# Layer-norm closings by full-array products at hand-set places, and 512-column products in the last feed-forward

## The chip, the cores and the metric

The kernel runs on one core of one Trainium2 chip. The metric is the device time of one execution in microseconds (us); less is better. A core has five engines with a queue of instructions each: TensorE (PE, matrix products), VectorE (DVE), ScalarE (ACT), GpSimd (POOL) and SyncE (SP, which here issues the DMA transfers). An engine works through its own queue in order, and waits at an instruction whose inputs, or whose buffers, aren't ready.

## The reference

Two layers of a transformer-like trunk over 256 context tokens and 256 latent tokens of width 1024. A layer is a SwiGLU feed-forward, a block of four token mixers in parallel, and a second feed-forward. Every one of these sub-layers is modulated and closed by a residual and a layer norm:

```
def modulate(h, mods, s):
    return h * (1 + mods[..., s, 1, :]) + mods[..., s, 0, :]
def residual(h, y, mods, s, g, b, r):
    return layer_norm(ALPHA * h + r * mods[..., s, 2, :] * y, g, b)
def swiglu_ffn(h, w_in, w_out):
    a = h @ w_in
    return (jax.nn.silu(a[..., :D_FF]) * a[..., D_FF:]) @ w_out
```

D_FF is 2816. All inputs are fp32, and only the latent tokens are returned, so the last sub-layers need the latent tokens alone.

## The kernel before

Channels lie on the 128 partitions and tokens along the free axis: eight tiles `ah[k]` of 128 channels by 512 columns hold the stream, columns 0 to 255 the context tokens (set 0), columns 256 to 511 the latent tokens (set 1). In the code `order` is (1, 0): the latent set comes first.

An fp32 product is made as three products in a faster format (fp32r). `split` turns a value into a rounded part and the rest: ScalarE writes `hi`, VectorE `lo`. A weight tile thus becomes `hi` and `lo`, an input tile `xh` and `xl` (in front of the first product of a sub-layer) or `gh` and its rest (in front of the second). `mm3` multiplies hi·hi, hi·lo and lo·hi into one PSUM tile; three such products are called a triple here. With both sets a triple has 512 columns, with one set 256. Split weights live in pools of six buffers (`hi`, `lo`), raw weights in four.

A feed-forward runs in three parts over 22 blocks of 128 hidden channels (`PARTS`). Per block it makes two product tiles of eight triples each (gate and up), then Silu on ScalarE, a product on VectorE and the split into `gh`. At the end of a part `out_tiles` multiplies the part's `gh` with the output weights into eight tiles, and `evac` adds each, times a gate, onto `ah[m]` (one `scalar_tensor_tensor`, `stt`, per set).

The layer norm is prepared while these last tiles arrive: `Norm.arrive` adds up the squares (`sq`) and the values (`lns`) of the eight tiles. `Norm.finish` closes it: products with a matrix of ones give the mean and the mean square of each token as rows (`st`, 32 equal rows per 128 tokens), ScalarE and VectorE work on a tile of 64 by 128 (`lnm`, `lnv`: copy, square, subtract, square root, reciprocal), and products with one column of the identity matrix, repeated, spread both rows over all 128 partitions (`bcm`, the mean, and `bcr`, the reciprocal deviation). Then `center` and `scale` on VectorE make the normalized tiles, ScalarE makes `xf` (the modulated tile), and the split gives `xh` and `xl`. `carry` multiplies `ah` for the next residual (the `ah<-ah,alg` instructions).

Between two sub-layers with both sets (four places: first feed-forward to mixers, mixers to second feed-forward, that to the next layer's first, and that to the second mixers) the last four output tiles are delayed (`LAG`): they are made for the latent set first, then for the context set (the late tiles), so that the latent closing lies beside the late tiles and the context closing beside the first products of the next sub-layer (the head). Behind the second mixers and behind the last feed-forward only the latent set is left, and the closing has no such company.

The order of instructions on each engine is set by the framework's scheduler, from the order in the code and its own costs.

Of the kernel before, what the change touches and what calls it, by code (L numbers as in the profile page):

```python
# [17 lines left out]
T = 256  # L18
# [16 lines left out]
HEAD = 3  # L35
PUMPS = ((3, 3), (3, 0), (3, 1))
# [24 lines left out]
def trunk_kernel(ctx: ExitStack, tc: tile.TileContext, I: dict, out: bass.AP):  # L61
# [81 lines left out]
    def mm3(ps, wh, wl, xh, xl, start, stop):  # L143
        mm(ps, wh, xh, start=start, stop=False)
        mm(ps, wh, xl, start=False, stop=False)
        mm(ps, wl, xh, start=False, stop=stop)
# [112 lines left out]
    class Norm:  # L259
# [3 lines left out]
        def __init__(self, n, tiles, pre=False):  # L263
            self.n, self.tiles, self.pre, self.bc = n, tiles, pre, {}

        def arrive(self, m, cs):
# [18 lines left out]
            if m == 0:  # L285
                self.q = sq
            else:
                if m == 1:
                    self.s = blk("lns")
                tt(out=self.q[:, cs], in0=self.q[:, cs], in1=sq[:, cs], op=ALU.add)  # L290
                tt(out=self.s[:, cs], in0=(self.tiles[0] if m == 1 else self.s)[:, cs], in1=d[:, cs], op=ALU.add)

        def finish(self, s):
# [3 lines left out]
            for i, x in enumerate((self.q, self.s)):  # L297
# [17 lines left out]

        def center(self, m, s, o):
# [7 lines left out]
    def xtiles():  # L324
        return ([xp.tile([128, 512], F32R, tag="xh", name=nm("xh")) for _ in range(8)],
                [xp.tile([128, 512], F32R, tag="xl", name=nm("xl")) for _ in range(8)])

    def start(mid):


        xh, xl = xtiles()
# [15 lines left out]
        for u in range(4):  # L347
# [15 lines left out]
            for k in (2 * u, 2 * u + 1):  # L363
# [15 lines left out]
                split(xh[k], xl[k], xf)  # L379
# [12 lines left out]
        return xh, xl, tiles  # L392
# [3 lines left out]
    class Boundary:  # L396
# [3 lines left out]
        def __init__(self, nrm, l, s, nl, ns_, keep, rest):  # L400
            self.nrm, self.ls, self.nx, self.keep, self.rest = nrm, (l, s), (nl, ns_), keep, rest
            self.xh, self.xl = xtiles()
            self.xf = {}

        def apply(self, v, ks):
            nrm = self.nrm
            c = vcols(v)
            for k in ks:
# [5 lines left out]
                split(self.xh[k][:, c], self.xl[k][:, c], xf[:, c])  # L414
# [16 lines left out]
        def prep(self, v):  # L431
            if v not in self.nrm.bc:
                self.nrm.finish(v)
                for k in range(HEAD):
                    self.nrm.center(k, v, ah[k])
                self.apply(v, range(HEAD))
                for k in range(HEAD, 8):
                    self.nrm.center(k, v, ah[k])
                for w, go in self.rest:
                    go()  # L440
                    self.nrm.finish(w)
                self.apply(v, range(HEAD, 8))
            else:
                for k in range(8):
                    self.nrm.center(k, v, ah[k])
                self.apply(v, range(8))

# [6 lines left out]
    def mmk(tiles, xh, xl, c):  # L454

        n = len(xh)
        for k in range(n):
            for p, wh, wl in tiles:
                mm3(p[:, c], ktile(wh, k), ktile(wl, k), xh[k][:, c], xl[k][:, c], k == 0, k == n - 1)

    def head_tiles(tiles, bd, order, cs):

        for v in order:
            if cs.start <= v * T:
                bd.prep(v)
                mmk(tiles, bd.xh, bd.xl, vcols(v))
        for v in order:
            if cs.start <= v * T:
                bd.carry(v)

    def out_tiles(load, gh, gl, cs, order, evac, lag):


        n = len(gh)
        for m in range(8 - lag):
            wh, wl = load(m)
            p = mmb()
            mmk([(p, wh, wl)], gh, gl, cs)
            evac(m, p, cs, order)
        late = []  # L480
# [3 lines left out]
        todo = []  # L484
        for i, v in enumerate(order if lag else ()):
            def go(v=v):
                for m, p, wh, wl in late:
                    mmk([(p, wh, wl)], gh, gl, vcols(v))
                    evac(m, p, vcols(v), (v,))

            if i:
                todo.append((v, go))
            else:
                go()
        return todo

    def resid(m, ps, l, s, sets):
# [26 lines left out]
    def ffn(l, w, bd, first, cs, order, np_, nm_=1):  # L524

        s = 2 * w
        nrm = Norm(1024, ah, True)
        xh, xl = first[:2] if bd is None else (bd.xh, bd.xl)
        rest = None
        for pi, (j0, j1) in enumerate(PARTS):  # L530
            gh, gl = [], []
            j = j0
            while j < j1:
                js = list(range(len(first[2]) // 2 if bd is None else 2)) if j == 0 else [j]
                tiles = first[2] if j == 0 and bd is None else ffn_tiles(l, w, js)
                if j == 0 and bd is not None:
                    head_tiles(tiles, bd, order, cs)
                elif j == 0:
                    mmk(tiles, xh, xl, cs)
                else:  # L540
                    for t in tiles:
                        mmk([t], xh, xl, cs)
                for i, jj in enumerate(js):
                    sg = blk("sg")
                    act(sg[:, cs], tiles[2 * i][0][:, cs], AF.Silu)
                    tt(out=sg[:, cs], in0=sg[:, cs], in1=tiles[2 * i + 1][0][:, cs], op=ALU.mult)
                    a, b = blk2("gh", cs, F32R)
                    split(a[:, cs], b[:, cs], sg[:, cs])
                    gh.append(a)
                    gl.append(b)  # L550
# [771 lines left out]
```

## Time and profile before

| what | value |
|---|---|
| median of 3 runs | 2264.93 us (2259.85 to 2268.72) |
| profiled execution | 2267.27 us, of which 2265.5 are the span of the trace |
| mean granted TensorE clock | 0.991 of full speed |
| VectorE busy | 1630.0 us, 72% of the span |
| ScalarE busy | 947.0 us, 42% |
| DMA | 323.23 MB, 143 GB/s on average |

The profile is of one execution. Busy time of an engine is the sum of its instructions; the span is from the first to the last instruction. Matmuls are pipelined: the duration of a row is longer than the distance to the next one, so the pace of products is read from their start times. A "granted clock" of 0.50 means that TensorE ran at 1.2 instead of 2.4 GHz in that stretch.

### The profile page before, as it was taken

How to read it: one execution, taken by the hardware profiler on the slowest of the kernel's cores; microseconds unless marked ns; L12 is line 12 of the kernel's file. 1: busy time of each engine (PE TensorE's matmuls, PEld its weight loads, DVE VectorE, ACT ScalarE, POOL GpSimd, SP SyncE). 2: the span in 40 equal slices, each digit the busy share in tenths (PEclk: the TensorE clock that was granted, in tenths of full speed). 3: DMA queues.
4: the chain of work that ended last, by engine and by line, in shares of the span. 5: the costliest groups of instructions: out<-in, count | busy, mean ns of one | idle time of the engine just before them, and what ended most of it. 6: DMA issues, size and time to landing. Idle time of an engine off the chain costs nothing.

```text
span 2265.5 us, 31565 instructions
## 1 busy us (share of the span) xinstructions
PE 2221.0 (98%) x12216; PEld 1908.4 (84%) x12216; DVE 1630.0 (72%) x2881; ACT 947.0 (42%) x1477; POOL 19.9 (1%) x82
## 2 busy tenths in 40 slices
PE   7999999999999999999999999999999999998997
PEld 4888788988888888898888888888889998998997
DVE  6998855768995754795746498766558988776656
ACT  5323123742345753362222254222226645755443
POOL 2000000000000000000000000000000000000000
PEclk9999999999999999999999999999999999999999
DMA  8676643223232132244545425554434543354652
GB/s 308 220 229 221 192 152 94 98 84 113 94 99 88 57 103 93 96 135 150 170 129 158 130 84 186 179 180 152 140 102 142 192 139 103 122 174 136 203 180 83
DMA packets 94454, 323.23 MB, mean 143 GB/s; under 512 B 10592, under 2 KB 12640, under 8 KB 94304
## 3 DMA queue, kind: packets, MB, share of 16 engines
q1 hardware_dynamic: 94304, 321.22, 43.9%
q8 instruction: 96, 1.57, 0.3%
q14 instruction: 54, 0.44, 0.1%
HBM read 320.12 MB, written 1.05 MB: 142 GB/s over the span
## 4 chain that ended last, share of the span: by engine, by line
PE 87%; DVE 7%; DMA 3%; issue 2%; ACT 2%; SPq 0%; DVEq 0%; ACTq 0%
PE mm L122 82%; DVE junk L216 2%; DMA ada<-in_wada 1%; DVE lo L113 1%; PE num L122 1%; DMA raw<-in_ffn_in 1%; DVE junk L366 1%; ACT hi L125 1%; DVE ah L113 0%; PE gt L122 0%; PE ax L122 0%; PE qk L122 0%; PE bcm L122 0%; PE bcr L122 0%; PE st L122 0%
## 5 line engine op out<-in xcount | busy, mean ns | idle before, releaser
L125 ACT ACTIVATE hi<-raw 128x1024 fp32r<-128x1024 f32 (+1 forms) x462 | 474.5, 1031 | 1040.0 <-PE mm L122 659.1
L122 PE MATMUL mm<-xh,hi 128*128 128x512 f32 (+1 forms) x2448 | 847.8, 349 | 5.0 <-ACT hi L125 3.0
L122 PE MATMUL mm<-xl,hi 128*128 128x512 f32 (+1 forms) x2448 | 850.0, 348 | 0.0
L122 PE MATMUL mm<-xh,lo 128*128 128x512 f32 (+1 forms) x2448 | 850.0, 348 | 0.0
L113 DVE TENSOR_TENSOR lo<-raw,hi 128x1024 fp32r<-128x1024 f32 (+1 forms) x462 | 546.2, 1185 | 264.6 <-ACT hi L125 262.4
L122 PEld LDWEIGHTS mm<-xh,hi 128*128 128x128 f32 x2448 | 462.4, 190 | 65.0 <-ACT hi L125 4.4
L122 PEld LDWEIGHTS mm<-xh,lo 128*128 128x128 f32 x2448 | 464.8, 190 | 58.8 <-DVE lo L113 0.4
L122 PEld LDWEIGHTS mm<-xl,hi 128*128 128x128 f32 x2448 | 465.2, 190 | 57.9 <-issue 0.7
L122 PE MATMUL mm<-gh,hi 128*128 128x512 f32 (+1 forms) x1600 | 405.8, 344 | 5.6 <-ACT gh L125 4.7
L216 DVE CUSTOM_DVE_ANT_0 junk<-ada,cbc 128x1024 bf16<-128x1024 f32 x256 | 312.9, 1222 | 107.1 <-DMA ada<-in_wada 104.0
L122 PEld LDWEIGHTS mm<-gh,hi 128*128 128x128 f32 x1600 | 276.6, 189 | 48.0 <-ACT gh L125 5.1
L122 PE MATMUL mm<-gh,lo 128*128 128x512 f32 (+1 forms) x800 | 275.5, 345 | 0.0
L122 PEld LDWEIGHTS mm<-gh,lo 128*128 128x128 f32 x800 | 150.8, 189 | 20.2 <-issue 0.7
L113 DVE SCALAR_TENSOR_TENSOR ah<-mm,gate,ah 128x256 f32<-128x256 f32 x192 | 86.4, 479 | 81.4 <-PE mm L122 81.2
L113 DVE SCALAR_TENSOR_TENSOR cacc<-pd,cw,cacc 128x512 f32<-128x512 f32 (+1 forms) x240 | 133.1, 613 | 0.2
L122 PE MATMUL mm<-yh,hi 128*128 128x512 f32 (+1 forms) x512 | 129.3, 339 | 0.1
L113 DVE TENSOR_TENSOR sg<-sg,mm 128x512 f32<-128x512 f32 (+1 forms) x87 | 53.7, 618 | 82.4 <-PE mm L122 81.7
L122 PEld LDWEIGHTS mm<-yh,hi 128*128 128x128 f32 x512 | 88.0, 189 | 11.6 <-ACT yh L125 0.3
L122 PE MATMUL mm<-yh,lo 128*128 128x512 f32 (+1 forms) x256 | 86.5, 338 | 0.0
L125 ACT ACTIVATE gh<-sg 128x512 fp32r<-128x512 f32 (+1 forms) x88 | 50.5, 574 | 76.0 <-DVE sg L113 75.5
L122 PE MATMUL mm<-mh,hi 128*128 128x256 f32 (+1 forms) x320 | 67.0, 306 | 0.5 <-ACT mh L125 0.3
L125 ACT ACTIVATE xf<-ah,bp,gp 128x256 f32<-128x256 f32 x88 | 48.8, 592 | 21.6 <-DVE ah L113 16.5
(241 smaller groups left out, 1759.6 us busy)
## 6 DMA issues: line engine op xcount, KB each, us to landing
raw<-in_ffn_in SPq DMA_DIRECT2D x176, 512.0 KB, 3.4
ada<-in_wada SPq DMA_DIRECT2D x136, 512.0 KB, 4.2
raw<-in_ffn_out SPq DMA_DIRECT2D x64, 512.0 KB, 3.7
raw<-in_w_G SPq DMA_DIRECT2D x64, 512.0 KB, 3.3
raw<-in_w_br SPq DMA_DIRECT2D x32, 512.0 KB, 3.3
raw<-in_ffn_out SPq DMA_DIRECT2D x32, 384.0 KB, 3.4
raw<-in_w_o SPq DMA_DIRECT2D x24, 512.0 KB, 3.4
shw<-in_wshift SPq DMA_DIRECT2D x16, 256.0 KB, 5.8
```

Of the source, the lines that this page charges most:

```text
L113: return f(*a, **k)
L122: nc.tensor.matmul(o, w, x, **kw)
L125: S.activation(o, i, f, **kw)
L216: V.tensor_tensor_reduce(out=cur["junk"], in0=w, in1=cur["c"][:, v], scale=1.0, scalar=0.0, op0=ALU.mult, op1=ALU.add, accum_out=m[:, v, t ...
L366: V.tensor_tensor_reduce(out=cur["junk"], in0=w, in1=cur["c"][:, v], scale=1.0, scalar=0.0, op0=ALU.mult, op1=ALU.add, accum_out=m[:, v, k ...
```

## The change

1. `finish` is replaced, between sub-layers and at the end, by `stats` and `spread` (the norm inside the mixers keeps `finish`). `stats` makes the mean by one product of the full ones matrix with `lns`, which leaves it on all partitions at once. The two sums per token are made with the tile as the weights and two columns of ones as the input, so that tokens lie on partitions; the square, the subtraction, the root and the reciprocal then work on a tile of 128 by 4 (`lnw`). Two `tensor_scalar` make a diagonal matrix of the result (`dg`), and `spread` multiplies it with the ones matrix.
2. Where only the latent set is left (`alone`), the last tile and its square are not added on VectorE but accumulated on TensorE as products of their own.
3. `head_tiles` writes the order of TensorE out by hand: after `GAP[0]` = 8 late triples `stats` of the latent set, 8 triples later `spread`, then the rest of the late triples; after 8 head triples `stats` of the context set, 8 later its `spread`.
4. In the last feed-forward the input tiles hold hi and lo side by side (`wide`), so hi·hi and hi·lo become one product of 512 columns; the two halves are added behind it, for gate and up by a copy on ScalarE and a sum on VectorE, for the output tiles by a second `stt`.

```
+        def stats(self, s):
+            n, cs = self.n, vcols(s)
+            b, c = aux("bcm"), aux("bcr")
+            for i, x in enumerate(self.s):
+                mm(b[:, 0:T], ones[n], x[:, cs], start=i == 0, stop=i == len(self.s) - 1)
+            ops = [(j, x, t) for i in range(len(self.q)) for j, x in ((0, self.q[i]), (1, self.s[i])) for t in range(2)]
+            for i, (j, x, t) in enumerate(ops):
+                o, k = T + 4 * j + 2 * t, s * T + t * 128
+                mm(c[:, o:o + 2], x[:, k:k + 128], ones[n][:, 0:2], start=i == 0, stop=i == len(ops) - 1)
+            e2, mu = c[:, T:T + 4], c[:, T + 4:T + 8]
...
+            act(v, mu, AF.Square)
+            tt(out=v, in0=e2, in1=v, op=ALU.subtract)
+            act(v, v, AF.Sqrt, bias=eps)
+            V.reciprocal(v, v)
+            dg = blk("dg")
+            for t in range(2):
+                ts(out=dg[:, t * 128:t * 128 + 128], in0=ident, scalar1=v[:, 2 * t:2 * t + 1], scalar2=float(n),
+                   op0=ALU.mult, op1=ALU.mult)
...
+        def spread(self, s):
+            mm(self.bc[s][1], ones[self.n], self.dg[:, 0:T], start=True, stop=True)
...
+        w, late = bd.rest
+        with tc.manual_schedule(engines={mybir.EngineType.PE}):
+            g = late()
+            some(g, GAP[0])
+            nrm.stats(v)
+            some(g, GAP[1])
+            nrm.spread(v)
...
+            for _ in g:
+                pass
+            bd.apply(v, range(HEAD, 8))
+            g = triples(tiles, xs, vcols(v))
+            some(g, GAP[0])
+            nrm.stats(w)
+            some(g, GAP[1])
+            nrm.spread(w)
...
+        if x.both is not None:
+            mm(ps, wh, x.both, start=start, stop=False)
+            mm(o, wl, hi, start=False, stop=stop)
...
+                    if wide:
+                        up = blk("up")
+                        for o, q in ((sg, 2 * i), (up, 2 * i + 1)):
+                            t = tiles[q][0]
+                            act(o[:, cs], t[:, 0:T], AF.Copy)
+                            tt(out=o[:, cs], in0=o[:, cs], in1=t[:, cs], op=ALU.add)
...
-            stt(out=ah[m][:, vcols(v)], in0=ps[:, vcols(v)], scalar=gate[l, s][:, v, m:m + 1],
-                in1=ah[m][:, vcols(v)], op0=ALU.mult, op1=ALU.add)
+            for c in ((vcols(0), vcols(v)) if wide else (vcols(v),)):
+                stt(out=ah[m][:, vcols(v)], in0=ps[:, c], scalar=gate[l, s][:, v, m:m + 1],
+                    in1=ah[m][:, vcols(v)], op0=ALU.mult, op1=ALU.add)
```

Three places show how the order moves. The first is the context closing between the first feed-forward and the mixers, on TensorE; `xh_2921` to `xh_2927` are input tiles of the latent set, `mm_` the head tiles (the change gives other numbers to the inputs: 2919, 2920, ... before, 2919, 2921, ... now). Before:

```order
L122 MATMUL mm_2972<-xl_2929,hi_2968 128x256
L122 MATMUL st_3132<-sq_2659,ones_81 32x128 x2
L122 MATMUL st_3132<-lns_2696,ones_81 32x128 x2
L122 MATMUL mm_2972<-xh_2921,lo_2969 128x256
...
L122 MATMUL mm_2958<-xl_2930,hi_2954 128x256
L122 MATMUL bcm_3139<-lnm_3137,ident 128x128 x2
...
L122 MATMUL mm_2972<-xh_2923,lo_2969 128x256
L122 MATMUL bcr_3140<-lnv_3138,ident 128x128 x2
L122 MATMUL mm_2951<-xh_2924,hi_2947 128x256
```

With the change:

```order
L123 MATMUL mm_2972<-xh_2921,lo_2969 128x256
L123 MATMUL bcm_3181<-lns_2696,ones_81 128x256
L123 MATMUL bcr_3182<-ones_81,sq_2659 128x2 x2
L123 MATMUL bcr_3182<-ones_81,lns_2696 128x2 x2
L123 MATMUL mm_2951<-xh_2923,hi_2947 128x256
...
L123 MATMUL mm_2972<-xh_2925,lo_2969 128x256
L123 MATMUL bcr_3182<-dg_3193,ones_81 128x256
L123 MATMUL mm_2951<-xh_2927,hi_2947 128x256
```

Three groups of products became two, with exactly eight triples between them; the second group stands ahead of the fifth input tile instead of behind the fifth.

The second place is ScalarE at the same boundary: `hi_` of a `raw_` is the split of a weight, `xf_` and `xh_` are the inputs of the latent set's head products, `lnm_3137`, `lnv_3138` and `lnw_3188` belong to the context closing. Before:

```order
L125 ACTIVATE xf_2994<-ah_102,bp_1294,gp_1293 128x256
L125 ACTIVATE hi_2968<-raw_2966 128x1024
L125 ACTIVATE xh_2919<-xf_2994 128x256
...
L125 ACTIVATE ah_104<-ah_104,alg_378 128x256
L125 ACTIVATE hi_3458<-raw_3456 128x1024
...
L125 ACTIVATE xf_3155<-ah_106,bp_1294,gp_1293 128x256
L125 ACTIVATE lnm_3137<-st_3132 64x128
L125 ACTIVATE xh_2923<-xf_3155 128x256
L125 ACTIVATE xf_3160<-ah_107,bp_1294,gp_1293 128x256
```

With the change:

```order
L126 ACTIVATE hi_2968<-raw_2966 128x1024
L126 ACTIVATE sq_3015<-ah_106 128x256
L126 ACTIVATE hi_3457<-raw_3455 128x1024
L126 ACTIVATE xf_3052<-ah_102,bp_1294,gp_1293 128x256
L126 ACTIVATE xf_3057<-ah_103,bp_1294,gp_1293 128x256
L126 ACTIVATE xh_2919<-xf_3052 128x256
...
L126 ACTIVATE xf_3152<-ah_109,bp_1294,gp_1293 128x256
L126 ACTIVATE lnw_3188<-bcr_3182 128x4
L126 ACTIVATE ah_105<-ah_105,alg_378 128x256
L126 ACTIVATE xh_2933<-xf_3152 128x256
L126 ACTIVATE lnw_3188<-lnw_3188,eps 128x4
```

The weight split of the next projection (`hi_3458`, now `hi_3457`) moved from behind the first three inputs to ahead of the first one, and the opening of the context closing from behind the fifth `xf` (`xf_3155`, of the tile `ah_106`) to behind the eighth.

The third place is ScalarE at the end of the first part of the last feed-forward, where the last block's gate (`sg`) and up values become `gh`; `mm_18027` and `mm_18034` are its two product tiles, `hi_` of 768 columns are splits of output weights. With the change:

```order
L126 ACTIVATE sg_18067<-mm_18027 128x256
L126 ACTIVATE hi_18164<-raw_18162 128x768
L126 ACTIVATE sg_18067<-sg_18067 128x256
L126 ACTIVATE hi_18185<-raw_18183 128x768
L126 ACTIVATE up_18068<-mm_18034 128x256
L126 ACTIVATE gh_18075<-sg_18067 128x256
```

Before, the same place read:

```order
L125 ACTIVATE hi_18261<-raw_18259 128x768
L125 ACTIVATE sg_18149<-mm_18093 128x256
L125 ACTIVATE hi_18287<-raw_18285 128x768
L125 ACTIVATE gh_18152<-sg_18149 128x256
L125 ACTIVATE hi_18313<-raw_18311 128x768
```

Two copies out of PSUM came in, and one more weight split now stands between the gate's copy and the last `gh`.

## Rows read from the trace of the kernel before

**Rows 1.** The page, first part: busy time, share of the span and instructions of each engine.
```profile
PE 2221.0 (98%) x12216; PEld 1908.4 (84%) x12216; DVE 1630.0 (72%) x2881; ACT 947.0 (42%) x1477; POOL 19.9 (1%) x82
```

**Rows 2.** Stretches: length; busy PE, PEld, DVE, ACT, POOL; granted clock; DMA share, GB/s.
```profile
22.20:25.80 3.60, 3.38 (x8) 2.46 (x9) 3.43 (x4) 2.41 (x5) 2.16 (x2) 0.53 1.04 386
398.00:426.00 28.00, 28.00 (x228) 26.28 (x227) 25.71 (x67) 21.52 (x47) 0.38 (x6) 1.00 0.12 39
2054.00:2062.00 8.00, 5.15 (x22) 4.86 (x23) 6.69 (x19) 5.38 (x13) 0.00 (x0) 0.50 0.13 51
```

**Rows 3.** Timeline of TensorE, last feed-forward: start, duration, engine, line, instruction, count.
```profile
2095.08 0.40 PE L122 MATMUL mm<-gh,hi 128*128 128x256 f32 x2
...
2096.86 0.96 PE L122 MATMUL mm<-gh,hi 128*128 128x256 f32 x4
2097.66 0.40 PE L122 MATMUL mm<-gh,lo 128*128 128x256 f32 x2
...
2149.90 0.28 PE L122 MATMUL mm<-xh,hi 128*128 128x256 f32 x1
...
2151.58 0.28 PE L122 MATMUL mm<-xh,lo 128*128 128x256 f32 x1
```

**Rows 4.** Timeline of TensorE, closings between first feed-forward and mixers.
```profile
401.72 0.71 PE L122 MATMUL bcr<-lnv,ident 64*128 64x128 f32 x4
402.36 0.38 PE L122 MATMUL mm<-gh,lo 128*128 128x256 f32 x1
...
414.28 0.41 PE L122 MATMUL st<-sq,ones 128*32 128x128 f32 x4
...
418.84 0.37 PE L122 MATMUL bcr<-lnv,ident 64*128 64x128 f32 x1
```

**Rows 5.** Timeline of ScalarE, same boundary.
```profile
404.42 1.06 ACT L125 ACTIVATE hi<-raw 128x1024 fp32r<-128x1024 f32 x1
405.39 0.40 ACT L125 ACTIVATE xh<-xf 128x256 fp32r<-128x256 f32 x1
405.70 1.08 ACT L125 ACTIVATE xf<-ah,bp,gp 128x256 f32<-128x256 f32 x2
406.68 0.71 ACT L125 ACTIVATE xh<-xf 128x256 fp32r<-128x256 f32 x2
407.30 1.57 ACT L125 ACTIVATE ah<-ah,alg 128x256 f32<-128x256 f32 x3
...
414.95 0.27 ACT L125 ACTIVATE lnm<-st 64x128 f32<-64x128 f32 x1
```

**Rows 6.** TensorE's waits, 18 to 26 us: who for what, total, times, longest.
```profile
PE mm L122 <- ACT hi L125: 2.5, 1, 2.5
```

**Rows 7.** Timeline of TensorE, 512-column products of the first feed-forward.
```profile
299.82 0.39 PE L122 MATMUL mm<-xh,hi 128*128 128x512 f32 x1
...
301.86 0.39 PE L122 MATMUL mm<-xh,hi 128*128 128x512 f32 x1
...
378.70 0.62 PE L122 MATMUL mm<-gh,hi 128*128 128x512 f32 x2
...
381.24 0.40 PE L122 MATMUL mm<-gh,lo 128*128 128x512 f32 x1
```

**Rows 8.** Timeline of all engines, the two one-set closings.
```profile
2049.43 0.28 PE L122 MATMUL mm<-mh,lo 128*128 128x256 f32 x1
...
2053.91 0.94 DVE L311 RECIPROCAL lnv<-lnv 64x128 f32<-64x128 f32 x1
...
2056.16 1.08 DVE L113 TENSOR_TENSOR ah<-ah,bcr 128x256 f32<-128x256 f32 x3 [0.71 <-PE bcr L122]
...
2058.07 1.22 PE L122 MATMUL mm<-xh,hi 128*128 128x256 f32 x4 [1.94 <-ACT xh L125]
...
2258.30 1.07 DVE L113 TENSOR_TENSOR ah<-ah,bcr 128x256 f32<-128x256 f32 x3
```

**Rows 9.** The products with `lf` in the mixers: what TensorE idled for, total, times.
```profile
  DVE lf L113: 4.2, 1
```

More of the change, by code (lines that the diff above doesn't have):

```diff
@@ L452, in ktile, with mmk, triples, some @@
         return w[:, k * 128:k * 128 + 128]
-    def mmk(tiles, xh, xl, c):
-        n = len(xh)
+    def mmk(tiles, xs, c):
+        for _ in triples(tiles, xs, c):
+            pass
+    def triples(tiles, xs, c):
+        n = len(xs)
         for k in range(n):
             for p, wh, wl in tiles:
-                mm3(p[:, c], ktile(wh, k), ktile(wl, k), xh[k][:, c], xl[k][:, c], k == 0, k == n - 1)
-    def head_tiles(tiles, bd, order, cs):
[L463 to L474, printed above, removed]
+                mm3(p, ktile(wh, k), ktile(wl, k), xs[k], c, k == 0, k == n - 1)
+                yield
+    def some(g, n):
+        for _ in range(n):
+            next(g, None)
+    def head_tiles(tiles, bd, order, cs):
+        nrm, xs = bd.nrm, bd.xs
+        v = order[0]
+        if not bd.rest:
+            nrm.stats(v)
+            nrm.spread(v)
+            for k in range(8):
+                nrm.center(k, v, ah[k])
+            bd.apply(v, range(8))
+            mmk(tiles, xs, vcols(v))
+            bd.carry(v)
+            return
+        w, late = bd.rest
+        with tc.manual_schedule(engines={mybir.EngineType.PE}):
+            g = late()
+            some(g, GAP[0])
+            nrm.stats(v)
+            some(g, GAP[1])
+            nrm.spread(v)
+            for k in range(8):
+                nrm.center(k, v, ah[k])
+            bd.apply(v, range(HEAD))
+            for _ in g:
+                pass
+            bd.apply(v, range(HEAD, 8))
[4 more added lines that the diff above has]
+            nrm.spread(w)
+            if cs.start <= w * T:
+                for k in range(8):
+                    nrm.center(k, w, ah[k])
+                bd.apply(w, range(8))
+            for _ in g:
+                pass
+            if cs.start <= w * T:
+                mmk(tiles, xs, vcols(w))
+        for u in order:
+            if cs.start <= u * T:
+                bd.carry(u)
+    def out_tiles(load, gs, cs, order, evac, lag):
         for m in range(8 - lag):
@@ L483, in out_tiles, with go, resid @@
             late.append((m, mmb(), wh, wl))
[L484 to L497, printed above, removed]
+        def go(v):
+            for m, p, wh, wl in late:
+                yield from triples([(p, wh, wl)], gs, vcols(v))
+                evac(m, p, vcols(v), (v,))
+        for _ in go(order[0]):
+            pass
+        return order[1], lambda: go(order[1])
+    def resid(m, ps, l, s, sets, wide=False):
         for v in sets:
[L499 to L500 removed]
+            for c in ((vcols(0), vcols(v)) if wide else (vcols(v),)):
+                stt(out=ah[m][:, vcols(v)], in0=ps[:, c], scalar=gate[l, s][:, v, m:m + 1],
+                    in1=ah[m][:, vcols(v)], op0=ALU.mult, op1=ALU.add)
     def ffn_tiles(l, w, js):
@@ L526, in ffn @@
         s = 2 * w
-        nrm = Norm(1024, ah, True)
-        xh, xl = first[:2] if bd is None else (bd.xh, bd.xl)
+        nrm = Norm(1024, ah, True, len(order) == 1)
+        xs = first[0] if bd is None else bd.xs
+        wide = xs[0].both is not None
         rest = None
         for pi, (j0, j1) in enumerate(PARTS):
-            gh, gl = [], []
+            gs = []
             j = j0
             while j < j1:
-                js = list(range(len(first[2]) // 2 if bd is None else 2)) if j == 0 else [j]
-                tiles = first[2] if j == 0 and bd is None else ffn_tiles(l, w, js)
+                js = list(range(len(first[1]) // 2 if bd is None else 2)) if j == 0 else [j]
+                tiles = first[1] if j == 0 and bd is None else ffn_tiles(l, w, js)
                 if j == 0 and bd is not None:
```

144 lines of the change are left out of this document (73 added, 71 removed).

## The prediction

> **What bounds the kernel now.** I read the page first: TensorE is busy for 98% of the span [rows 1], so time is won or lost only where TensorE waits or where its own products get cheaper. Then I read the stretches: around a two-set closing TensorE is busy for all 28.0 us while VectorE has 25.71 of them and ScalarE 21.52 [rows 2]; such a closing costs no wait today, but little slack is left on the other engines. Around the one-set closing behind the second mixer TensorE is busy for 5.15 of 8.0 us, at a granted clock of 0.50 [rows 2]. Last I read the timelines of the products and of the closings, for prices.
>
> **Sum to be made.** The profiled execution took 2267.27 us, 2265.5 of them span; the median of the runs is 2264.93. Everything below is a difference, so I add it to the profiled execution for the trace and to the median for the forecast.
>
> **Two-set closings, order.** There are four, all with the same code. I count in us from the end of the first late tile of the context set. A triple of 256-column products costs about 0.355 us: 15 products take 1.78 us from 2095.08 to 2096.86 [rows 3]. Eight triples are 2.8 us. For `stats` I take 1.6 (one 256-column fp32 product, four of two columns; the nearest rows are the old closing's: its last two products hold TensorE from 401.72 to 402.36 [rows 4]), for `spread` 0.7. TensorE then reads: `stats` of the latent set 0 to 1.6, second tile to 4.4, `spread` to 5.1, third tile to 7.9, fourth to 10.8, eight head triples to 13.6, `stats` of the context set to 15.2, eight more to 18.1. There it wants `dg` of the context set.
>
> ScalarE decides when `dg` is there. In the order of the change the weight split `hi_3457` stands ahead of the first `xf` of the latent set. The pool of split weights has six buffers, and this split takes the one that the third late tile reads, so it starts at 7.9. Behind it, up to the Square that opens the context closing, stand one more weight split, eight `xf`, seven `xh`, three `ah`, two `sq` and a `dmy`. By starts on ScalarE a split takes 0.97 us, an `xf` and an `ah` 0.49, an `xh` 0.31 [rows 5]; with `sq` as `xh` and 0.2 for `dmy` that is 2×0.97 + 11×0.49 + 9×0.31 + 0.2 = 10.3, so the Square starts at 18.2. The square root stands behind one `ah` and one `xh` more (19.2), then come the reciprocal and two `tensor_scalar` between other work on VectorE: `dg` at about 20.8. TensorE waits 20.8 − 18.1 = **2.7 us**. Before, the same distance on TensorE (414.28 to 418.84) was enough [rows 4], because the copy that opens the closing ran 0.67 us after its products began [rows 4, 5]. Bounds: 0 if ScalarE is 2.7 us ahead of this count (the split's buffer free when it asks); 3.7 if VectorE, the fuller engine, adds a microsecond. The walk is nearest to 2.7, so I take that. For the fourth closing the scheduler leaves eight triples of another projection between `stats` and `spread`, so the count there is 2.7 − 2.8, nearly level; I take 0.7 for its error. Sum: 3×2.7 + 0.7 = **+8.8**. Behind this TensorE wait stand the remaining head products, nothing else; the next closing's data are hundreds of microseconds away, so it isn't given back.
>
> **The clock after such a wait.** The only wait of this length that stands alone in the trace is 2.5 us on a weight split [rows 6], and the 3.6 us after it ran at 0.53 [rows 2]: 3.6×0.47 = 1.7 us lost. Whether a wait at full speed between full tiles does the same, no row shows. I take one fall in three, **+1.7**, with 0 and three times 1.7 as ends. The Trainium skill, page "TensorE: Matmul & The Clock Gate", section "Loop structure matters more than you think", says that matmuls which follow long waits run on the slow clock while back-to-back ones keep the fast one; by that rule these closings are the place where the change could lose twice. The trace agrees at the places just named.
>
> **Products of the closings.** The old one has three groups of four products, the last of 0.64 us [rows 4]; with a tenth of a microsecond on either side for the change between the formats (an estimate, from the products not fitting closer there) that is 2.4, and the new one takes 1.6 + 0.7. Eight closings give **−1.0**. Ends: 0 and −3.
>
> **Last feed-forward, products.** Each of its 352 `xh` triples (22 blocks × 2 × 8) and 176 `gh` triples (22 × 8) turns two 256-column products into one of 512. Today 14 products of the `xh` form take 1.68 us, 0.120 each [rows 3]; nine of the 512-column form take 2.04, 0.227 each, and eleven of `gh` 2.54, 0.231 each [rows 7]. So an `xh` triple goes from 0.360 to 0.347, a `gh` triple (0.118 a product, 15 of them in the 1.78 us above) from 0.354 to 0.349: 352×0.013 + 176×0.005 = **−5.4**. If the lone product loses pace beside a wide one it is −3.5, if `gh` runs like `xh`, −6.2. The Trainium skill, same page, section "Wait — 56ns, not 53.3ns?", puts a fixed 2.5 ns on top of the columns at 2.4 GHz, so that 528 products fewer would give 1.3 us and the forecast would be 4 us higher. The trace disagrees on the size: 0.227 where the page has 0.2157, and 13 ns between two of 256 and one of 512.
>
> **Last feed-forward, the two halves.** Per block ScalarE gets two copies and VectorE two sums; per output tile VectorE gets a second `stt`. Inside a part, 5.5 us of products per block cover these. At a part's end they don't: TensorE needs the last `gh` after only the other blocks' triples, and already today four products take 0.80 us at that point instead of 0.47 [rows 3]. Copy, sum and their hand-overs add about 0.65 us; in the first part a weight split of 768 columns now stands ahead of the last copy on ScalarE and its `lo` ahead of the sum on VectorE, which makes it 1.6. Sum 1.6 + 0.5 + 0.5 = **+2.6** (ends 0.9 and 3.5).
>
> **One-set closings.** Behind the second mixer, 8.64 us lie between the start of the last output product and the first head product [rows 8]. The reciprocal of 0.94 us on the way shrinks to some 0.15 and the two sums of `sq` and `lns` (by durations like those of one `ah` scaling, a third of a microsecond each) go; eight records of two columns and two `tensor_scalar` come. I get the scaling to start 1.5 us earlier than 2056.16 [rows 8]. But the first head product is now wide and needs `xl` too, which comes after five scalings: 7.4 us in all, **−1.2**. The clock falls anyway, 0.50 in this stretch [rows 2]. The final closing has the same chain (the reciprocal there too) with a second `stt` of 0.4 us in its way, scaled from 2258.30 on today [rows 8]: **−1.2**. Ends of each: 0 and −2.5.
>
> **Mixers.** The scheduler orders their small products differently too, with the same work. Their one long wait, 4.2 us for `lf` in the second mixer [rows 9], keeps its chain and its place. I take 0, ends ±4.
>
> **Sum.** 8.8 + 1.7 − 1.0 − 5.4 + 2.6 − 1.2 − 1.2 = **+4.3**: 2271.6 for the profiled execution, **2269.2** against the median.
>
> **Rivals.**
> - *Forecast, chance 0.50*: the context closings stall TensorE by 2 to 3.5 us in three places, and gains and losses elsewhere nearly cancel: 2264 to 2276.
> - *No stall, 0.25*: ScalarE is ahead, because `hi_3457` finds its buffer early or the `xf` don't fill the time. For it: it has 6.5 us idle in the 28 of [rows 2]. Against: the order of its queue is fixed, and the split can't pass the third late tile. Without 8.8 and 1.7 the time is 2258.7; with the better ends of the feed-forward (−6.2, +0.9) 2256.2; with both one-set closings at −2.5 as well, 2253.6, which is where a measurable gain begins.
> - *The clock falls at each stall, 0.20*: three falls, and a wait of 3.7 each. For it: [rows 6] and the 0.53 behind it. Against: that wait came in the start of the program, behind products of another kind. 2269.2 + 2×1.7 + 3×1.0 = 2275.6; at the price of the stretch behind the second mixer, where 5.15 us of products at 0.50 cost half their time, 2.6 [rows 2], each fall adds 0.9 more, and the time is 2278.3. It is measurably slower from the point where the three falls cost 2 us each on top of the full waits.
> - *The mixers move by more than their ends, or the wide products gain nothing, 0.05*.
>
> **Numbers.** 2269.2 is the first case's. The range leaves out the far end of the second case and what lies beyond the third's 2278.3 plus the mixers' 4: 2254 to 2282. A measurement of this kernel tells about 0.5% from no change, 11.3 us: below 2253.6 lies a part of the second case, since several of its ends can come together, and half of the last, 0.14; above 2276.3 two thirds of the third, half of the last and a little of the first, 0.19; the rest is 0.67. In the first case alone: 2264 to 2276.
>
> **What would show it.** In the changed profile: a TensorE wait of 2 to 3.5 us ahead of `bcr<-dg` in the context closings and none ahead of the latent ones; the opening Square on ScalarE some 3 us after its products; a granted clock below 1.0 right behind; 512-column pace of 0.227 to 0.232 in the last feed-forward; longer waits at its three part ends, the first the longest; 7 to 7.5 us between the second mixer's last product and the first head product. It is wrong if TensorE meets `dg` ready, if the stalls bring long slow stretches, or if the last feed-forward's pace differs from the sum by more than 2 us.

## The result: 0.7% slower, and the profile after

The changed kernel takes 2280.41 us (median of 4 runs, 2279.24 to 2283.01); the kernel before took 2265.8 us beside it (4 runs, 2259.85 to 2268.72). The ratio is 1.0069, with a 95% interval of 1.0047 to 1.0092. The profiled execution has a span of 2277.8 us against 2265.5, so 12.3 us are to be explained. The page's first part of the changed kernel, which answers to [rows 1]:

```profile
PE 2221.1 (98%) x11668; PEld 1885.8 (83%) x11668; DVE 1648.9 (72%) x2955; ACT 953.8 (42%) x1517; POOL 18.8 (1%) x82
```

TensorE is busy as long as before (2221.0 there), with 548 products fewer. So, in the balance, the 12.3 us are time in which it waited. To find where, I compared the start of the same instruction, counted from the beginning, in both traces: up to the last feed-forward, the n-th `stt` onto `ah` is the same piece of work in both. The difference grows like this:

| up to (us in the trace before) | after minus before | step |
|---|---|---|
| end of the first feed-forward, 388 | +0.8 | +0.8 |
| first `lf` product of the first mixers, behind the first closing | +2.9 | +2.1 |
| end of the first mixers, 935 | +4.5 | +1.6 |
| end of the second feed-forward, 1303, behind the second closing | +6.5 | +2.0 |
| end of the next one, 1694, behind the third closing | +7.9 | +1.4 |
| second mixers' output tiles, 2031, behind the fourth closing | +17.4 | +9.5 |
| the closing behind the second mixers: last output product to first head product, 8.64 to 8.73 | | +0.1 |
| the last feed-forward: first head product to last `gh` product, 192.92 to 188.92 | | −4.0 |
| last `gh` product to the end, 14.50 to 13.30 | | −1.2 |

The steps add up to 12.3. The first of them is no effect: until 388 us both kernels do the same, and in the profiles of this study that stretch differs from the one before by −2.0 to +1.9. Two things stand out: some 2 us at each of three closings, and 9.5 us in one stretch, the fourth closing with the second mixers.

**The closings of the context set.** TensorE at the first of them (columns as in [rows 4]):

```profile
413.19 0.59 PE L123 MATMUL bcm<-lns,ones 128*128 128x256 f32 x2
413.62 0.50 PE L123 MATMUL bcr<-ones,sq 128*128 128x2 f32 x4
413.98 0.59 PE L123 MATMUL bcr<-ones,lns 128*128 128x2 f32 x4
414.43 0.36 PE L123 MATMUL mm<-xh,hi 128*128 128x256 f32 x1
...
417.26 0.28 PE L123 MATMUL mm<-xh,lo 128*128 128x256 f32 x1
419.97 0.67 PE L123 MATMUL bcr<-dg,ones 128*128 128x256 f32 x2 [2.43 <-DVE dg L114]
```

`stats` holds TensorE from 413.19 to 414.43, eight triples follow, and then it stands for 2.43 us until `dg` is there. The list of TensorE's waits from 380 to 1420 us puts three such closings into its first line (total, times, longest):

```profile
PE bcr L123 <- DVE dg L114: 7.3, 3, 2.5
```

ScalarE at the same place, which answers to [rows 5]:

```profile
412.99 1.04 ACT L126 ACTIVATE hi<-raw 128x1024 fp32r<-128x1024 f32 x1
413.94 1.08 ACT L126 ACTIVATE xf<-ah,bp,gp 128x256 f32<-128x256 f32 x2
414.93 0.71 ACT L126 ACTIVATE xh<-xf 128x256 fp32r<-128x256 f32 x2
...
417.14 0.59 ACT L126 ACTIVATE xf<-ah,bp,gp 128x256 f32<-128x256 f32 x1
417.63 0.15 ACT L126 ACTIVATE lnw<-bcr 128x4 f32<-128x4 f32 x1
...
418.48 0.28 ACT L126 ACTIVATE lnw<-lnw,eps 128x4 f32<-128x4 f32 x1
```

The Square (`lnw<-bcr`) takes 0.15 us but starts 4.4 us after `stats` began: it stands behind the last of the eight `xf`. The root follows at 418.48, `dg` at 419.35 on VectorE. At the fourth closing the wait is 0.36.

Stretches behind these three waits, three places of the second mixers, and the one-set closing behind them (columns as in [rows 2]):

```profile
417.00:425.00 8.00, 5.57 (x45) 5.34 (x44) 7.50 (x25) 7.59 (x20) 0.00 (x0) 1.00 0.01 2
985.00:993.00 8.00, 5.55 (x45) 5.32 (x44) 7.29 (x24) 7.59 (x20) 0.00 (x0) 1.00 0.01 2
1358.00:1365.00 7.00, 4.57 (x37) 4.34 (x37) 6.32 (x21) 6.60 (x18) 0.00 (x0) 1.00 0.01 2
1753.00:1760.00 7.00, 6.92 (x46) 6.92 (x46) 4.15 (x8) 3.45 (x7) 0.00 (x0) 0.77 0.63 217
1768.00:1775.00 7.00, 3.11 (x15) 2.50 (x15) 3.84 (x9) 4.58 (x12) 0.00 (x0) 0.87 0.48 150
1775.00:1780.00 5.00, 5.00 (x37) 5.00 (x37) 3.04 (x8) 2.06 (x5) 0.00 (x0) 0.84 0.00 0
2069.00:2077.00 8.00, 3.29 (x13) 2.32 (x13) 7.26 (x24) 3.79 (x11) 0.00 (x0) 0.57 0.28 87
```

In this execution the granted clock stays at 1.00 behind the waits at the closings; in that of another kernel below, with the same waits at the same places, it doesn't. In the second mixers it is 0.77 to 0.87, where the kernel before has 1.00 (its stretches 1753 to 1760 and 1768 to 1780). In these three stretches that is at most 7×0.23 + 7×0.13 + 5×0.16 = 3.3 us (an estimate).

**The second mixers.** TensorE's waits from 1700 to 1790 us; the kernel before has none there:

```profile
PE ax L123 <- ACT dh L126: 3.6, 2, 2.3
PE mm L123 <- ACT yh L126: 1.6, 1, 1.6
PE ax L123 <- DVE dh L114: 0.9, 1, 0.9
...
```

`dh` is the split result of the pooling branch: VectorE adds `pd` up, makes `dp` from it, ScalarE rounds it. VectorE in the changed kernel:

```profile
1743.44 1.21 DVE L114 TENSOR_TENSOR lo<-raw,hi 128x1024 fp32r<-128x1024 f32 x1
1744.58 0.42 DVE L114 TENSOR_TENSOR pd<-pd 128x261 f32<-128x261 f32 x1
1744.92 2.35 DVE L114 TENSOR_TENSOR lo<-raw,hi 128x1024 fp32r<-128x1024 f32 x2
...
1747.53 0.41 DVE L114 TENSOR_TENSOR dp<-pd 128x256 f32<-128x256 f32 x1
1747.86 1.21 DVE L114 TENSOR_TENSOR lo<-raw,hi 128x1024 fp32r<-128x1024 f32 x1
...
1749.45 1.23 DVE L114 TENSOR_TENSOR lo<-raw,hi 128x1024 fp32r<-128x1024 f32 x1
1750.59 0.42 DVE L114 TENSOR_TENSOR dp<-dp,pd 128x256 f32<-128x256 f32 x1
```

ScalarE at the end of that chain, and TensorE behind it:

```profile
1751.66 1.06 ACT L126 ACTIVATE hi<-raw 128x1024 fp32r<-128x1024 f32 x1 [2.25 <-DMA raw<-in_w_G]
1752.63 0.40 ACT L126 ACTIVATE dh<-dp 128x256 fp32r<-128x256 f32 x1
```

```profile
1753.08 0.58 PE L123 MATMUL ax<-dh,pwh 128*128 128x256 f32 x1 [2.26 <-ACT dh L126]
```

Weight splits (`lo`, `hi`) of 1.1 to 1.2 us each now stand between the small steps of the pooling branch, and the last of them had itself waited 2.25 us on ScalarE for its weights. From its first `pd` to `dh` it takes 13.3 us (1739.37 to 1752.63); before it took 7.0 (1729.39 to 1736.35). The products with `dh` stand at their place in TensorE's queue, so TensorE waits 2.26 us. With two more for later `dh` and one for `yh`, a later split on ScalarE, the four long waits come to some 6.2 us; with the 3.3 us of slower clock that is about the whole of the 9.5.

**The last feed-forward and the one-set closings.** TensorE, a part's end and eight pairs of products with `xh`, which answer to [rows 3]:

```profile
2114.57 0.28 PE L123 MATMUL mm<-gh,lo 128*128 128x256 f32 x1
2114.91 0.50 PE L123 MATMUL mm<-gh,hi 128*128 128x512 f32 x1
2115.25 0.28 PE L123 MATMUL mm<-gh,lo 128*128 128x256 f32 x1
...
2139.93 0.40 PE L123 MATMUL mm<-xh,hi 128*128 128x512 f32 x1
2140.17 0.28 PE L123 MATMUL mm<-xh,lo 128*128 128x256 f32 x1
...
2142.76 0.40 PE L123 MATMUL mm<-xh,hi 128*128 128x512 f32 x1
```

Eight triples take 2.83 us, 0.354 each; over the second and third part it is 0.353 (0.237 for the wide product, 0.117 for the other), against 0.360 before. In the first part, once the clock is back at 1.00, it is 0.347 (0.230 and 0.117). At the part's end one lone and one wide product take 0.68 us (2114.57 to 2115.25) where their pace gives 0.35: 0.33 more, as much as in [rows 3], where four products take 0.80 instead of 0.47. TensorE at the closing behind the second mixers (answers to [rows 8]):

```profile
2066.87 0.28 PE L123 MATMUL mm<-mh,lo 128*128 128x256 f32 x1
...
2071.48 1.19 PE L123 MATMUL bcr<-dg,ones 128*128 128x256 f32 x2 [1.79 <-DVE dg L114]
2075.59 0.80 PE L123 MATMUL mm<-xh,hi 128*128 128x512 f32 x1 [2.92 <-DVE xh L114]
```

VectorE there:

```profile
2071.25 2.06 DVE L114 TENSOR_TENSOR ah<-ah,bcm 128x256 f32<-128x256 f32 x6
2073.24 1.73 DVE L114 TENSOR_TENSOR ah<-ah,bcr 128x256 f32<-128x256 f32 x5
2075.12 0.76 DVE L114 TENSOR_TENSOR xh<-xf,xh 128x256 fp32r<-128x256 f32 x2
```

The scaling starts 6.37 us after the last output product (before 6.73): `spread` is through at 2072.67, 5.8 us after it, and for the rest the centerings, which now all stand ahead, hold VectorE. The wide head product needs the half that VectorE writes behind five scalings.

### The profile page after: what moved, and what is told of

It is laid out like the page before. It is cut to its first block, busy times and chain, and to the rows that moved or that the text cites. A ratio compares the mean times of both kernels' runs of the same rounds, so it can differ in the third digit from the quotient of the medians.

```text
span 2277.8 us, 30559 instructions
## 1 busy us (share of the span) xinstructions
PE 2221.1 (98%) x11668; PEld 1885.8 (83%) x11668; DVE 1648.9 (72%) x2955; ACT 953.8 (42%) x1517; POOL 18.8 (1%) x82
## 4 chain that ended last, share of the span: by engine, by line
PE 84%; DVE 7%; DMA 3%; ACT 3%; issue 2%; SPq 0%; DVEq 0%; ACTq 0%
PE mm L123 79%; DVE junk L236 2%; DVE lo L114 1%; DMA ada<-in_wada 1%; DMA raw<-in_ffn_in 1%; PE num L123 1%; ACT hi L126 1%; DVE junk L422 1%; ACT xf L126 1%; DVE ah L114 1%; PE bcr L123 1%; PE ax L123 1%; PE gt L123 0%; ACT xh L126 0%; PE qk L123 0%
## 5 line engine op out<-in xcount | busy, mean ns | idle before, releaser
L123 PE MATMUL mm<-xh,hi 128*128 128x512 f32 (+1 forms) x2448 | 879.4, 366 | 6.3 <-ACT hi L126 3.1
L123 PE MATMUL mm<-xl,hi 128*128 128x512 f32 (+1 forms) x2096 | 752.3, 359 | 0.0
L123 PEld LDWEIGHTS mm<-xl,hi 128*128 128x128 f32 x2096 | 397.2, 190 | 58.0 <-issue 0.9
L123 PEld LDWEIGHTS mm<-gh,hi 128*128 128x128 f32 x1424 | 255.1, 188 | 56.0 <-ACT gh L126 6.4
L114 DVE SCALAR_TENSOR_TENSOR ah<-mm,gate,ah 128x256 f32<-128x256 f32 x216 | 97.1, 479 | 79.4 <-PE mm L123 78.8
L114 DVE TENSOR_TENSOR gh<-sg,gh 128x512 fp32r<-128x512 f32 (+1 forms) x88 | 54.4, 618 | 1.7 <-ACT gh L126 1.7
```

The source lines that it names most:

```text
L114: return f(*a, **k)
L123: nc.tensor.matmul(o, w, x, **kw)
```

## The experiments

Two theories were to be told apart for most of the 12 us. **A, the closings**: the hand-set places of `spread` come before `dg` can be there, and what follows is their consequence. **B, the planner**: the mixers have a planner of their own. `pump` hands out steps of the branches as long as

```
while tasks and work["v"] * SLOW[l] < work["pe"] + lead[0]:
```

where `work` adds up estimated times of everything issued so far, the closing's products included, and `LEAD` is a table of leads per step. By the code's own prices the old closing counted eight products of 128 columns at 1.69 ns a column, 1730 ns; the new one counts 879. Two closings stand in each mixer's count, so TensorE's count is 1.70 us lower (VectorE's 0.11), and the side work gets 1.6 us less of lead. By this theory its steps are issued later, behind more weight splits, though the chip takes no longer for any of them.

**No wide products**, the change without point 4:

```
-    bd = Boundary(nrm, 1, 1, 1, 2, (1,), rest, True)
+    bd = Boundary(nrm, 1, 1, 1, 2, (1,), rest)
```

> The change without its wide tiles: the last feed-forward runs as in the kernel before, all closings as in the change. Theory: the wide products gain about 5 us and their part ends and the later first product cost about 2, so this is 3 to 4 us slower than the change, 2283 to 2285 (ratio to before 1.008). Rival, that the wide tiles bring nothing or cost time: 2280 or less. In the profile the 14.6 us loss should stand in the same places as in the change, ahead of the last feed-forward.

2280.8 us, ratio 1.0061 (1.0048 to 1.0075). The slowdown stays, so it isn't made in the last feed-forward. In the trace the feed-forward takes 192.84 us instead of 188.92 and the closing ahead of it 8.27 instead of 8.73, so in the traces the wide products win 3.5 us; the timed runs don't resolve this here (the intervals overlap).

**`spread` 16 triples behind `stats`** in the context closings:

```
             nrm.stats(w)
-            some(g, GAP[1])
+            some(g, 16)
             nrm.spread(w)
```

> The change with the spread of the context set 16 instead of 8 triples behind its stats, at all four two-set boundaries. Theory: the three waits of 2.45 us ahead of it come from TensorE asking 2.5 us too early; 8 more triples (2.9 us) cover them, so 7 us less: about 2273. Rival, that the wait only moves to the first products that need the context set: 2279 to 2281. The waits at the start of the second mixers should stay.

2271.9 us, 1.0025 (1.0015 to 1.0035). The waits for `dg` are gone, and the three closings together add nothing up to 1694 us (+0.7 against the trace before, where the change has +7.9). Up to the `lf` products of the second mixers, the measure for these mixers from here on, it still adds 7.4 us (the change 9.7), with the waits of the change. So A is shown for its part, and for that alone.

**The old closings and the old order at the two-set places**; the one-set closings and the wide products stay as in the change:

```
-        with tc.manual_schedule(engines={mybir.EngineType.PE}):
...
+        nrm.finish(v)
...
+        nrm.finish(w)
```

> Only the one-set closings and the wide tiles of the change; the four two-set boundaries have the closings and the free order of the kernel before. Theory: the whole loss is in the two-set boundaries and behind them; what is left gains about 4 us in the last feed-forward and 1 at the end, 2260 to 2262 (ratio 0.998). Rival, that the rest of the change loses too: 2266 or more.

2263.07 us, 0.9985 (0.9976 to 0.9993). All of the slowdown comes with the two-set closings, the mixers' share too: the difference to the trace before is +1.1 up to 1694 us and +0.6 up to 2031. The one-set closings and the wide products alone win 0.15%.

**The fourth closing's order left to the scheduler**, its instructions as in the change:

```
-        with tc.manual_schedule(engines={mybir.EngineType.PE}):
+        with nullcontext() if cs.start else tc.manual_schedule(engines={mybir.EngineType.PE}):
```

> The change, but at the fourth two-set boundary (to the second mixers) the order of TensorE is left to the scheduler. Theory: the waits of 6 us at the start of the second mixers, and the slow clock behind them, come from the order that stands there (weight splits ahead of the pooling chain) and part of it goes: 2272 to 2277. Rival, that the order by hand has no part in it: 2280.

2277.46 us, 1.0047 (1.0035 to 1.006). The second mixers still add 5.3 us, and the pooling branch still takes 12.2 us from its first `pd` to `dh` (13.3 in the change). The hand-written order of that closing is a part of their loss, not most of it.

**The lead given back**: 1.6 added to every entry of `LEAD`, the closings as in the change.

```
-LEAD = ((-3, -19, -18, -14, -28, -19, -4, 28, 1), (0, -2, 0, 0, -5, 0, 0, 37, -4))
+LEAD = ((-1.4, -17.4, -16.4, -12.4, -26.4, -17.4, -2.4, 29.6, 2.6), (1.6, -0.4, 1.6, 1.6, -3.4, 1.6, 1.6, 38.6, -2.4))
```

> The change with all entries of LEAD raised by 1.6. Theory: inside the mixers a planner emits side work by two counters of work, PE and VectorE; the new closings count 1.70 us less of PE and 0.11 us less of VectorE there, so that all side work (the pooling chain first) comes 1.6 us later in the program and behind more weight splits on ScalarE and VectorE. Raised by as much, the waits for dh at the start of the second mixers (6 us with the slow clock behind them) mostly go, and 1 us in the first mixers: 2271 to 2275. Rival A, that the load of pool_w behind two weight loads on the DMA queue is the cause: it stays there in this kernel, so 2279 to 2281. Rival B, that the order by hand at the fourth boundary is: 2280 too.

2275.35 us, 1.0042 (1.0029 to 1.0055). The first mixers, which cost 1.6 us in the change, now win 0.3 (from +1.9 to +1.6 over the stretch), and the second add 6.1 instead of 9.7. From the first `pd` to `dh` it takes 7.8 us instead of 13.3. The waits in the second mixers, from 1700 to 1790:

```profile
PE ax L123 <- ACT dh L126: 2.1, 2, 1.6
PE mm L123 <- ACT yh L126: 2.0, 1, 2.0
...
```

So B is shown as a cause of its own, and it doesn't explain all of the second mixers. The lead was not raised in the kernel before, so whether a part of the gain has nothing to do with the new closings stays untested; the first mixers come back to about their time in the kernel before (0.3 less). The load of the pooling weights, which the change moved on SP's queue behind two more weight loads (issued at 1731.66 instead of 1712.34), stays behind them here, and the first `dh` costs TensorE only 0.55 us all the same; the load is not what makes it 2.26 us late. A later `dh` still costs 1.56.

The three waits at the closings stay at 7.3 us here, 2.43 to 2.45 each, but the clock behind them doesn't stay at 1.00. Stretches behind them in this trace:

```profile
418.00:426.00 8.00, 7.92 (x53) 7.78 (x53) 7.14 (x18) 7.07 (x18) 0.00 (x0) 0.80 0.05 9
987.00:995.00 8.00, 8.00 (x54) 7.95 (x55) 7.67 (x19) 7.59 (x20) 0.00 (x0) 0.79 0.12 33
1360.00:1367.00 7.00, 7.00 (x46) 6.82 (x46) 6.24 (x17) 6.17 (x16) 0.00 (x0) 0.77 0.01 4
```

TensorE falls to the lower level, 1.2 GHz, behind each of the three. By the places of the table the three closings add 9.0 us here and 5.5 in the change: some 1.2 us for each fall. In the kernel without wide products and in the one with the free fourth closing, which have the same three waits, it falls behind the third alone. Around these waits TensorE, ScalarE and VectorE go through the same instructions in the same order in all four kernels, so the order of the work doesn't decide whether the clock falls; what does, no run settles.

**The Square ahead of four inputs**, `spread` at its place of the change:

```
-            bd.apply(v, range(HEAD, 8))
+            bd.apply(v, range(HEAD, 4))
             g = triples(tiles, xs, vcols(v))
...
             nrm.stats(w)
+            bd.apply(v, range(4, 8))
             some(g, GAP[1])
```

> The change, but the inputs 5 to 8 of the first set are written in the code behind stats of the second set, so that on ScalarE its Square stands behind the fourth xf instead of the eighth and the root before the fifth. TensorE's order is the same in the first three boundaries. Theory: the 2.45 us waits are ScalarE's queue ahead of the Square, so they go, 7 us less: 2272 to 2275. Rival, that VectorE or the inputs behind it are as late: the wait stays, or moves to the fifth input tile, 2278 to 2281.

2270.86 us, 1.0019 (1.001 to 1.0028), as good as moving `spread` (1.0025). ScalarE at the first closing:

```profile
414.75 0.58 ACT L126 ACTIVATE xf<-ah,bp,gp 128x256 f32<-128x256 f32 x1
415.41 0.17 ACT L126 ACTIVATE lnw<-bcr 128x4 f32<-128x4 f32 x1
...
416.28 0.28 ACT L126 ACTIVATE lnw<-lnw,eps 128x4 f32<-128x4 f32 x1
```

The Square runs behind the fourth `xf`, 2.2 us earlier, and TensorE doesn't wait for `dg` at any of the three. So the place in ScalarE's queue caused the stall; the distance on TensorE is the other end of the same account.

**Both repairs**: the lead with `spread` at 16, and the lead with the Square ahead. Their edits are those shown above.

> LEAD raised by 1.6 and the spread of the second set after 16 triples. Theory: the two losses are independent, so this is the run with spread after 16 alone (2271.9) less 6: 2264 to 2267. Rival, that they overlap: 2269 or more.

> LEAD raised by 1.6 and the inputs 5 to 8 behind stats of the second set. Theory: 2265 to 2268, as the run with LEAD and 16 triples. Faster than the kernel before (2264 or less) only if the new closings gain where they no longer wait.

2262.64 us, 0.9984 (0.9975 to 0.9993), and 2262.92 us, 0.9984 (0.9975 to 0.9993). From 1.0069 that is 0.85%; the single steps give 0.44% or 0.50% (the closing's repairs) and 0.27% (the lead), so the two causes add up, to 0.71 or 0.77%, and the rest is within the intervals. (The falls of the clock behind the closings, 3.5 us in the one trace with the lead alone, go with the waits too, which may be the rest.) By the same places as in the table a two-set closing now wins 0.7 to 1.2 us (in the first of the two kernels from +1.5 to +0.4 at the first closing). The second mixers still add 3.8 and 4.3 us; in the first kernel's trace TensorE waits there 2.0 us for `yh` and twice, 1.2 us together, for `dh`, and has a granted clock of 0.82 from 1753 to 1760.

**The lead and `spread` at 16, without the wide products.**

> The kernel with LEAD raised and the second set's spread after 16 triples, without the wide tiles. Theory from the traces (the offset to the kernel before falls by about 4 us between the start and the end of the last feed-forward with wide tiles, and stays level without): 3 to 4 us slower than with them, 2266 (ratio to before 1.000). Rival, from the timed runs with and without wide tiles, which differed by 0.4 us: 2263.

2264.97 us, 0.999 (0.9981 to 0.9999). Against the same kernel with wide products (0.9984) the timed difference is within the intervals; in the traces the wide products win 4.8 us here.

**The old fourth closing**: new closings at three places with `spread` at 16, the lead raised for the first mixers alone, wide products kept.

```
+        if cs.start:
+            nrm.finish(v)
...
+            nrm.finish(w)
...
+            bd.carry(v)
+            return
```

> LEAD raised for the first mixers alone, the second set's spread after 16 triples in three boundaries, and the old closings with the free order at the fourth. Theory: what is left at the start of the second mixers (2 to 3.5 us in the run with LEAD and 16 triples) comes with the closings by hand there and goes: 2258 to 2261 (ratio 0.9970). Rival, that it comes from elsewhere: 2262 to 2264.

> The same kernel as the run with the old closings at the fourth boundary, to stand on one chip beside its twin without wide tiles. If the last result holds: ratio to before 0.996, about 9 us.

2258.18 us, 0.9963 (0.9951 to 0.9975), and the same kernel on another chip 2259.15 us, 0.9969 (0.9957 to 0.9981). TensorE has no wait from 1700 to 1790 us, and the second mixers add 0.1 us. It is faster than both kernels: 0.3 to 0.4% below the one before.

**The same without the wide products**, on the chip of the repetition:

> That kernel without the wide tiles. Theory from the traces: the wide tiles are worth 3.5 to 4 us, so this is slower than its twin on the same chip by that much (ratio to before 0.9980). Rival from the timed pairs so far (0.4 and 1.4 us, on different chips): within 1.5 us of it.

2261.03 us, 0.998 (0.9971 to 0.9989). On the same chip the wide products are worth 1.9 us by the medians, with intervals that overlap a little: neither the 3.5 to 4 of the theory nor the rival's 1.5 or less. TensorE without them, first head product and last product of the last feed-forward, and with them:

```profile
2054.92 0.80 PE L123 MATMUL mm<-xh,hi 128*128 128x256 f32 x2 [2.46 <-ACT xh L126]
...
2248.02 0.28 PE L123 MATMUL mm<-gh,lo 128*128 128x256 f32 x1
```

```profile
2055.65 0.80 PE L123 MATMUL mm<-xh,hi 128*128 128x512 f32 x1 [2.93 <-DVE xh L114]
...
2244.25 0.28 PE L123 MATMUL mm<-gh,lo 128*128 128x256 f32 x1
```

193.1 us become 188.6, and the closing ahead gives 0.47 of it back (8.27 to 8.74): 4.0 in the traces against 1.9 in the medians. The three pairs of traces have 3.5, 4.8 and 4.0; the size is not settled better than that.

## Why the prediction was wrong in its likeliest case

The time, 2280.41, lies inside the range (2254 to 2282), but the forecast was 2269.2, "same" had 0.67 and measurably slower 0.19; it became slower by 0.69%. That it lies inside the range is luck: the mixers, whose ends were ±4, cost some 11 us, and gains elsewhere hid a part. Step by step:

- **Two-set closings, order: right.** The walk through ScalarE's queue gave 4.6 us from the start of `stats` to the Square, 4.4 were measured; the three waits are 2.43, 2.45 and 2.43 instead of 2.7, the fourth 0.36 instead of 0.7. That is 7.7 of 8.8. The two experiments that move either end of this distance show the cause.
- **The clock after such a wait: nothing in this execution, instead of 1.7; a fair guess over all.** The granted clock is 1.00 behind all three here. Behind the same waits in three other kernels it fell five times in nine, at some 1.2 to 1.5 us a fall where 1.7 was forecast, so "one fall in three" was no bad estimate. The rival that put the slow end of the range there had the right size by a mechanism that did not act in this execution. By the rule of the Trainium skill (page "TensorE: Matmul & The Clock Gate", section "Loop structure matters more than you think") these waits should have cost clock; this trace doesn't show it there, the trace with the raised lead does at all three (0.77 to 0.80). In the second mixers, behind the wait of 2.26 us, the granted clock is 0.77.
- **Products of the closings: mis-sized, inside the ends.** With the stalls gone each place with two closings wins 0.7 to 1.2 us, three places some 3; the forecast had 1.0 for four places (end −3). `stats` takes 1.24 us (413.19 to 414.43) where 1.6 was taken.
- **Last feed-forward, products: right for one pace, mis-sized for another.** −5.4 was forecast. A triple of the `xh` form takes the forecast 0.347 in the first part and 0.353 in the other two; the `gh` form takes 0.350, with 0.349 forecast. By these paces 96×0.013 + 256×0.007 + 176×0.004 = 3.7 us (an estimate), close to the text's lower end of 3.5. The wide product's own pace changes, 0.230 or 0.237, beside the same lone one: with the raised lead all three parts run at 0.347 (seven triples in 2.43 us below), and the feed-forward takes 187.22 us. What sets it, no run here shows.

```profile
2135.80 0.39 PE L123 MATMUL mm<-xh,hi 128*128 128x512 f32 x1
...
2138.23 0.39 PE L123 MATMUL mm<-xh,hi 128*128 128x512 f32 x1
```

- **The two halves: +2.6 was wrong, nearly nothing came.** The first part's end takes no more than before (0.33 us over the pace, as in [rows 3]), so the copies and sums are covered there. Products and halves together gave −4.0 where −2.8 was forecast.
- **One-set closings: one wrong, one right.** Behind the second mixers +0.1 instead of −1.2: the reciprocal did shrink, but `spread` and the centerings ahead of the scaling let it start only 0.4 us earlier instead of 1.5, and the wide product waits for VectorE. The final one gave −1.2 as forecast.
- **Mixers: this is the step that failed.** It took 0, ends ±4, since the same work was only ordered differently and the long wait for `lf` keeps its chain. The measured +1.6 and some 9.5 (with 0.4 of closing) are more than all the rest. The order of the change shows the pooling branch behind more weight splits; I costed a list of moved instructions at nothing without following the chain that runs through them (`pd`, `dp`, `dh`, then TensorE). What moved them was the planner's count, which the cheaper closing lowers by 1.6 us: the lead alone returns 1.9 us in the first mixers and 3.5 in the second, and shortens the chain from 13.3 us to 7.8.

The last rival, the mixers beyond their ends, had 0.05. What stays open: of the second mixers' loss 3.8 us remain with the lead given back and no stalls ahead of it (4.3 with the other repair), and they vanish with the old fourth closing. How they divide between its fixed order and the shifted place of the pooling weights' load was not tried apart.

## What to carry to other kernels

A closing that becomes cheaper also changes the books of a planner that counts it: list what else reads the count, and follow each dependent chain whose steps moved in an engine's queue, past every weight split, until an engine that is full waits for it. A distance set by hand on one engine must be checked against the queue of the engine that closes the loop; moving four inputs behind one small instruction on that queue was worth as much as doubling the distance. Judge the parts of a mixed change apart: here, with the distance and the first mixers' lead put right, three closings, the wide products and the final closing win, the fourth closing loses with its mixers, and the mixture without it is 0.3 to 0.4% faster than the kernel before. Look at more than one trace before a clock or a pace is put down to the code: the same waits kept the full clock in one execution and lost it in another.

## What the hardware showed

A wait of 2.4 us among full 256-column products doesn't settle the clock behind it: in the profiled execution of the change three such waits left the granted clock at 1.00, and with the raised lead the same three, at the same places, stand ahead of stretches at 0.80, 0.79 and 0.77. A wait of 2.26 us among the mixers' products stands ahead of a stretch at 0.77, the wait of 2.5 us of [rows 6] ahead of one at 0.53.

A 512-column product beside one of 256 has a pace of 0.237 us in some parts of the last feed-forward and 0.230 in others, with the same instructions, against 0.227 among its own kind [rows 7]; so a single stretch doesn't tell what a wider product saves.
